# Token rows for the experts: turned a PSUM bank at a time, and the first pair's tokens by products

## The chip, the cores and the metric

One core of one Trainium2 chip runs the whole layer. The time is the device time of one execution in microseconds, as the median of several runs; 1143.99 us before the change (three runs, 1141.77 to 1146.23). Engines are named as the profile names them: PE (TensorE, products), PEld (its weight loads), DVE (VectorE), ACT (ScalarE), POOL (GpSimd), SP (SyncE, which here only issues transfers).

## What is computed

One layer of a backbone over 512 latent tokens of width 1024 (batch 1, depth 1). After the first half (retention, long convolution, merging and output projection) comes the part that matters here, the routed experts:

```
h2 = modulate(rms_norm(x, norm2_g), sh2, sc2)              # 512 x 1024
group_p = softmax(h2 @ rg_w + rg_b);  g = argmax            # 4 groups of 8 experts
in_group = the 8 logits of that group;  top 2 of softmax    # two experts for each token
y[token] = sum over its 2 experts of weight * (silu(u @ w1[e]) * (u @ w3[e])) @ w2[e]     # hidden 512
x = x + gt2 * y;  out = rms_norm(x, final_norm_g)
```

All is f32. The 32 experts' weights are 32 x 3 x 2 MB, about 201 MB, and each is read once.

## The kernel before

**Experts in pairs, pairs in groups.** The 32 experts make 16 pairs, two pairs to a group `g` (0 to 7). An expert takes up to 64 tokens in a round (`CAP`), so a pair is 128 slots: 64 of its first expert, 64 of its second. For a pair, `up_half` makes the two hidden products (`ga` with w1, `up` with w3) from the pair's tokens in columns `xg` (feature on the partition, slot along the row), `hidden` gates them, `turned` transposes the result into `hT`, `down` makes `y`, and `add` puts weighted results back to the tokens with a one-hot matrix (`co`). In the trace an f32 product or transpose of the code is two rows or one: 20 warm-up products are 40 rows, 4 transposes 4 rows, 8 products of 64x512 16 rows.

**Where the tokens come from.** `rows_of` and `chosen` build `gtm`, one-hot rows (token to slot) for the four experts of a group. `slot_sums` multiplies it with token numbers and the tokens' norm factor, `fetched` makes an index of that and fetches 128 rows of the token stream from HBM into `xr[j]` with an indirect DMA (POOL), and `scaled` multiplies each row by its token's norm factor (half on DVE, half on ACT). `token_columns` (line 1492) turns `xr` into `xg`: it transposes blocks of 128 features on PE into a PSUM bank `xg`, and after each block (one pair) or each two (two pairs) a DVE or ACT instruction, in turns, takes it out with the modulation (`am2c`, `sh2c`). So one bank is written, read, written again, and read by the other engine.

**Order of the work.** A stretch from the last output products to the first pair's tokens (`tail()` to line 1644) stands in program order on all engines (`order = tc.manual_schedule()`). From line 1667 on, PE alone keeps program order, and a scheduler orders the other engines. At the first pair the two fetches are waited for on PE with `keep_warm` products; `xr[0]` is turned, the first half of `up_half` runs, `xr[1]` is turned, the second half runs. In each group from 0 to 6 the turn for the next group's two pairs stands on PE behind the second pair's `up` and behind `turned(hh)`, ahead of the second pair's `down`.

**The weights' transfers.** `plan` lists 192 tiles of 1 MB (12 for a pair: 8 for `up`, 4 for `down`), and `ahead(n)` issues them on SP in that order as buffers come free. The buffers are 12 ring tiles (`ew`) and loans: two tiles in the former `xm`, one in two halves (`xwxe`, the second half in the pool `late`, which takes the place of the routing's scratch when that is closed), one `xwxf`; in all 16 tiles in flight or in use. A tile's buffer is free when its products are done. In group 5 a check for experts with more than 64 tokens stands in the program (`overflow`), which SP also passes.

Of the kernel before, what the change touches and what calls it, by code (L numbers as in the profile page):

```python
# [48 lines left out]
W = 4, 2, 1, 10, 2, 8  # L49
# [124 lines left out]
def body(es: ExitStack, tc: tile.TileContext, d, out, dump=None):  # L174
# [15 lines left out]
    def bank(name, tag="x"):  # L190
        return ps.tile([128, 512], F32, name=name, tag=tag, bufs=4)

    def f(t):
        return t.bitcast(F32)
# [59 lines left out]
    def run(gen):  # L254
        for _ in gen:
            pass
# [26 lines left out]
    def early_table(func, src):  # L283

        A.activation(junk1, src, func, scale=0.0)
# [953 lines left out]
    rl, sq = [], []  # L1239

    def out_tile(o, k):
        xk = xm[k // 2][:, k % 2, :]
        V.scalar_tensor_tensor(out=xk, in0=o, scalar=gt1c[:, k:k + 1], in1=xk, op0=ALU.mult, op1=ALU.add)
        s = wide("sq2")[:, 0:512]
        A.activation(s, xk, AF.Square)
        sq.append(s)
        if 0 < k < 7:
            V.tensor_tensor(out=s, in0=sq[0], in1=s, op=ALU.add)
            sq.pop(0)
# [76 lines left out]
    def tail():  # L1326
# [13 lines left out]
        early_table(AF.Sqrt, sq[-1][:, 0:1])  # L1340
        ss = bank("ss")
# [7 lines left out]
        V.tensor_tensor(out=lgt_v, in0=lgt_v, in1=rl[2][:, 0:160], op=ALU.add)  # L1349
        for j in range(2):  # L1350
            for t in range(4):
                T.matmul(ss[:, 4 * j + t:4 * j + t + 1], sq[j][:, 128 * t:128 * t + 128], ones[:, 0:1], start=True, stop=True)
        V.tensor_reduce(out=mtmp, in_=ss[:, 0:8].rearrange("p (j t) -> p t j", j=2), axis=AX.X, op=ALU.add)
# [3 lines left out]
        rsqrt_mean(mrs, mtmp, 1024, mtmp, mss)  # L1357
# [133 lines left out]

    def token_columns(xg, pairs, c0=0):

        w = 128 * len(pairs)
        for k in range(8):
            i = w * k % 512
            if i == 0:
                p = bank("xg")
            for j, pr in enumerate(pairs):
                T.transpose(p[:, i + 128 * j:i + 128 * j + 128], xr[pr][:, 128 * k:128 * k + 128], ident)  # L1500
            o = xg[k][:, c0:c0 + w]
            if k % 2:
                A.activation(o, p[:, i:i + w], AF.Identity, bias=sh2c[:, k:k + 1], scale=am2c[:, k:k + 1])  # L1503
            else:
                V.tensor_scalar(out=o, in0=p[:, i:i + w], scalar1=am2c[:, k:k + 1], scalar2=sh2c[:, k:k + 1],  # L1505
                                op0=ALU.mult, op1=ALU.add)
# [86 lines left out]
    def overflow():  # L1593
# [3 lines left out]
        with tc.If(rounds > 1, label="more"):  # L1597
            with tc.For_i(1, rounds, 1):
                V.tensor_scalar(out=later, in0=later, scalar1=float(CAP), scalar2=None, op0=ALU.add)
                with tc.For_i(0, 16, 1) as pi:  # L1600
# [9 lines left out]
                    token_columns(xg, [0])  # L1610
# [17 lines left out]
    def rows_of(g):  # L1628
        gt = wk.tile([128, 4, 4 * CAP], F32R, name="gtm", tag="gt", bufs=1)
        return gt, chosen(gt, pos[:, :, 4 * g:4 * g + 4], 4, slots, 2)  # L1630

    gt, more = rows_of(0)
    xg = column_tiles(4, "m")
    rs = []
    for j in range(2):
        next(more)
        rs.append(fetched(slot_sums(gt, 128 * j, wHL[:, :, j, 4:8]), j))
    weights_ = shares()
    next(weights_)
    keep_warm(W[5])  # L1640
    scaled(rs[0], 0)
    token_columns(xg, [0])
# [38 lines left out]
    for g in range(8):  # L1681
# [7 lines left out]
        if g == 0:  # L1689
            ab_ = [bank("ga", "acc"), bank("up", "acc")]  # L1690
            up_half(ab_, 0, xg, 0, ahead_weights)
            scaled(rs[1], 1)
            token_columns(xg, [1], 128)
            run(weights_)
# [10 lines left out]
            rs = []  # L1705
# [25 lines left out]
        if g == 0:  # L1731
            gt, more = rows_of(1)
            run(more)
            nxt = described(1, gt)
# [7 lines left out]
        if g < 7:  # L1742
            for j in range(2):
                scaled(rs[j], j)
            hT_ = turned(hh)
            xg = column_tiles(4, "m")
            token_columns(xg, [0, 1])
            parts.append((now[1][0], down(hT_, now[1][1], ahead_weights)))
# [121 lines left out]
```

## Time and profile before

| | |
|---|---|
| median of 3 runs | 1143.99 us |
| the profiled execution: its own time | 1140.63 us |
| its span, first to last instruction | 1138.9 us |
| PE, DVE, ACT busy | 95%, 51%, 30% of the span |
| moved by DMA | 289.48 MB |
| mean granted TensorE clock | 0.965 of 2.4 GHz |

The page gives busy time, slices and groups; a row of the timeline gives the start and the length of an instruction or of a run of like ones, and in brackets how long its engine was idle before it and what ended that. A matmul's end is modelled, so a PE that reads as fully busy may still be waiting a little. The span is 1.7 us shorter than the execution's own time, which is 3.4 us below the median.

### The profile page before, as it was taken

What the parts mean: (1) busy time and instruction counts of PE and PEld (TensorE: products, weight loads), DVE (VectorE), ACT (ScalarE), POOL (GpSimd) and SP (SyncE); (2) the same over time, 40 slices, a digit from 0 to 9 for tenths busy, and PEclk for the clock granted to TensorE, in tenths of its full rate; (3) what the DMA queues carried; (4) which work ended last, traced back from release to release, by engine and by line L of the source; (5) the groups of instructions that cost most, each with busy time, mean ns of one, the idle gap of its engine ahead of it and who ended that gap; (6) DMA issues with size and microseconds to landing.
All of it is one profiled execution on the core that took longest, in us unless ns stands there. A gap on an engine that the chain in (4) does not pass through costs nothing. (4 is left out here: it accounts for less than half of the span.)

```text
span 1138.9 us, 13047 instructions
## 1 busy us (share of the span) xinstructions
PE 1077.3 (95%) x4958; PEld 675.8 (59%) x4958; DVE 579.5 (51%) x1045; ACT 337.9 (30%) x588; POOL 41.1 (4%) x68
## 2 busy tenths in 40 slices
PE   6999999999999999999998798989898989898996
PEld 3667888877778777877888233534353434343343
DVE  1778995775475768865535241424243324233234
ACT  2487352445533455333332211111101010101113
POOL 0010000000000000000002000000000000000000
PEclk8999999999999999999998798989998989999899
DMA  7653343111122128883599489999999998999971
GB/s 267 197 175 110 111 142 127 62 56 60 55 91 74 38 78 298 262 274 106 199 420 397 165 314 366 418 417 415 418 416 418 417 409 351 415 417 418 418 305 74
DMA packets 64925, 289.48 MB, mean 254 GB/s; under 512 B 8086, under 2 KB 10262, under 8 KB 45274
## 3 DMA queue, kind: packets, MB, share of 16 engines
q1 hardware_dynamic: 59818, 274.51, 62.9%
q0 software_dynamic: 5040, 14.10, 3.6%
q8 instruction: 40, 0.66, 0.2%
q14 instruction: 27, 0.22, 0.1%
HBM read 288.57 MB, written 4.19 MB: 257 GB/s over the span
## 5 line engine op out<-in xcount | busy, mean ns | idle before, releaser
L198 DVE TENSOR_TENSOR wL<-raw,wH 128x512 fp32r<-128x512 f32 x142 | 97.1, 688 | 118.9 <-ACT wH L197 110.3
L197 ACT CAST wH<-raw 128x512 fp32r<-128x512 f32 x142 | 87.9, 621 | 206.6 <-PE ro L202 33.7
L1534 PE MATMUL up<-ew,xgm 128*64 128x512 f32 x496 | 111.7, 592 | 0.0
L1559 PE MATMUL y<-ew,hT 128*64 128x512 f32 x368 | 105.2, 653 | 1.0 <-DVE hT L1548 1.0
L1534 PE MATMUL ga<-ew,xgm 128*64 128x512 f32 x280 | 93.4, 619 | 0.0
L1540 DVE TENSOR_TENSOR hh<-hh,up 128x512 f32<-128x512 f32 x16 | 11.0, 688 | 135.5 <-PE up L1534 135.5
L1534 PEld LDWEIGHTS up<-ew,xgm 128*64 128x64 f32 x496 | 35.3, 137 | 71.2 <-issue 69.7
L1559 PEld LDWEIGHTS y<-ew,hT 128*64 128x64 f32 x368 | 31.5, 151 | 50.1 <-issue 48.6
L1500 PE MATMUL xg<-ident,xr 128*128 128x128 f32 x128 | 29.5, 339 | 29.5 <-DVE xgm L1505 24.6
L1490 ACT ACTIVATE xr<-xr,rs 128x512 f32<-128x512 f32 x16 | 11.5, 722 | 152.5 <-DMA xr<-rows,idx 152.5
L1565 DVE SCALAR_TENSOR_TENSOR yv<-y,wsl,gt 128x512 f32<-128x512 f32 x30 | 22.4, 747 | 64.2 <-PE y L1559 59.9
L197 ACT CAST yh<-yv 128x512 fp32r<-128x512 f32 x30 | 18.5, 618 | 104.2 <-DVE yv L1565 92.5
L1582 DVE TENSOR_TENSOR xmid<-xmid,co 128x512 f32<-128x512 f32 x58 | 39.8, 688 | 12.5 <-PE co L1574 11.9
L1574 PE MATMUL co<-yh,cmb 128*128 128x512 f32 x114 | 46.1, 405 | 0.0
L1574 PE MATMUL co<-yl,cmb 128*128 128x512 f32 x114 | 44.8, 393 | 0.0
L1534 PEld LDWEIGHTS ga<-ew,xgm 128*64 128x64 f32 x280 | 28.4, 144 | 24.0 <-issue 24.0
L1503 ACT ACTIVATE xgm<-xg,sh2c,am2c 128x256 f32<-128x256 f32 (+1 forms) x36 | 19.4, 540 | 77.7 <-PE xg L1500 77.7
L1500 PEld LDWEIGHTS xg<-ident,xr 128*128 128x128 f32 x128 | 16.3, 160 | 41.3 <-DVE xgm L1505 34.4
L342 DVE SCALAR_TENSOR_TENSOR acc<-adaw,scT,acc 128x1024 f32<-128x1024 f32 x28 | 35.6, 1282 | 8.7 <-DMA adaw<-ada 8.7
L1489 DVE TENSOR_SCALAR xr<-xr,rs 128x512 f32<-128x512 f32 x16 | 7.8, 486 | 60.9 <-DMA xr<-rows,idx 60.9
L1539 ACT ACTIVATE hh<-ga 128x512 f32<-128x512 f32 x16 | 9.6, 598 | 91.4 <-PE ga L1534 87.2
L1505 DVE TENSOR_SCALAR xgm<-xg,am2c,sh2c 128x256 f32<-128x256 f32 (+1 forms) x36 | 18.4, 512 | 32.8 <-PE xg L1500 32.8
(476 smaller groups left out, 2400.8 us busy)
## 6 DMA issues: line engine op xcount, KB each, us to landing
ew<-w SPq DMA_DIRECT2D x146, 1024.0 KB, 14.8
raw<-w_in SPq DMA_DIRECT2D x52, 512.0 KB, 3.7
xwxm<-w SPq DMA_DIRECT2D x40, 512.0 KB, 13.6
adaw<-ada SPq DMA_DIRECT2D x32, 512.0 KB, 6.0
xwxe<-w SPq DMA_DIRECT2D x22, 512.0 KB, 16.4
xwxf<-w SPq DMA_DIRECT2D x10, 1024.0 KB, 16.4
adaw<-ada SPq DMA_DIRECT2D x32, 256.0 KB, 6.0
raw<-ret_w_o SPq DMA_DIRECT2D x8, 512.0 KB, 3.7
```

What stands on the lines that cost most here:

```text
L197: A.copy(h, src)
L198: V.tensor_tensor(out=l, in0=src, in1=f(h), op=ALU.subtract)
L342: V.scalar_tensor_tensor(out=acc[i], in0=w, scalar=scT[:, k, 0:1], in1=acc[i], op0=ALU.mult, op1=ALU.add)
L1490: A.activation(xr[j][:, 512:1024], xr[j][:, 512:1024], AF.Copy, scale=rs)
L1500: T.transpose(p[:, i + 128 * j:i + 128 * j + 128], xr[pr][:, 128 * k:128 * k + 128], ident)
L1503: A.activation(o, p[:, i:i + w], AF.Identity, bias=sh2c[:, k:k + 1], scale=am2c[:, k:k + 1])
L1505: V.tensor_scalar(out=o, in0=p[:, i:i + w], scalar1=am2c[:, k:k + 1], scalar2=sh2c[:, k:k + 1], op0=ALU.mult, op1=ALU.add)
L1534: T.matmul(ab_[i][64 * e:64 * e + 64], xg[k][:, c0 + 64 * e:c0 + 64 * e + 64], w[e][q], start=(k == 0), stop=(k == 7))
L1559: T.matmul(y_[n][64 * e:64 * e + 64], hT_[:, 128 * k + 64 * e:128 * k + 64 * e + 64], w[e][2 * q + n], start=(k == 0), stop=(k == 3))
L1565: V.scalar_tensor_tensor(out=yv, in0=y_[n], scalar=wsl, in1=gt2[:, ns], op0=ALU.mult, op1=ALU.mult)
L1574: T.matmul(p, cmb[:, 128 * t:128 * t + 128], y[j][:, ns], start=(start and i + j == 0), stop=(i == len(parts) - 1 and j == 1))
L1582: V.tensor_tensor(out=xmid[:, t, ns], in0=xmid[:, t, ns], in1=p, op=ALU.add)
```

## The change

1. `token_columns` makes all transposes of one PSUM bank, and only then takes the bank out, all of it by one engine: banks 0 and 3 by DVE, 1 and 2 by ACT (one pair: bank 0 DVE, bank 1 ACT). It is now a generator that yields after each bank.
2. In groups 0 to 6, three of the four banks are turned ahead of `turned(hh)`, the fourth behind it.
3. The first pair's tokens are not fetched. DVE multiplies the pair's one-hot rows by the tokens' norm factor (`gs`, two instructions of 128x256, held in `xr[0]`), and PE multiplies the token stream `xmid` with them: 8 blocks of 4 f32 products of 128x128 into 4 banks, which DVE and ACT take out in turns. The `keep_warm` products that waited for the fetch are gone.
4. The second pair's rows are fetched as before, but their index is made between the second and the third bank of these products; they are turned only behind the first pair's `down`.
5. In `tail()` the squares' sums are added to the end on DVE, so 4 products make the sum over features and no DVE sum of two halves is left; one addition of router logits moves into the wait for the square root.

On PE at the first pair (`xr_5098` and `xr_5094` are `xr[0]`, `xr_5099` is `xr[1]`), before:

```order
L251 MATMUL warm<-ones 128x128 x4
L1475 MATMUL wsl<-wHL,gtm 128x4 x8
L251 MATMUL warm<-ones 128x128 x16
L1500 MATMUL xg<-ident,xr_5098 128x128 x8
L1534 MATMUL ga<-ew,xgm 64x512 x8
L1534 MATMUL up<-ew,xgm 64x512 x8
L1500 MATMUL xg<-ident,xr_5099 128x128 x8
L1453 LDWEIGHTS ones_b
```

and now:

```order
L251 MATMUL warm<-ones 128x128 x4
L1651 MATMUL xg<-xr_5094,xmid 128x128 x16
L1473 MATMUL wsl<-wHL,gtm 128x4 x4
L1651 MATMUL xg<-xr_5094,xmid 128x128 x16
L1451 LDWEIGHTS ones_b
...
L1538 MATMUL ga<-ew,xgm 64x512 x8
L1538 MATMUL up<-ew,xgm 64x512 x8
L1538 MATMUL ga<-ew,xgm 64x512 x8
```

The 32 products stand where the index products, 16 warm-up products and 8 transposes stood, and no transpose stands between the halves of the first pair's `up` any more.

On PE at a group's turn (here of group 1; the tiles by number, so that the four banks `xg` can be told apart; `xr0`, `xr1` hold the two pairs' rows), before:

```order
L1534 MATMUL up_5515<-ew_5281,xgm_5165 64x512
L1546 MATMUL hT_5555<-ident_61,hh_5548 128x128 x4
L1500 MATMUL xg_5564<-ident_61,xr0_5098 128x128
L1500 MATMUL xg_5564<-ident_61,xr1_5099 128x128
...
L1500 MATMUL xg_5585<-ident_61,xr0_5098 128x128
L1500 MATMUL xg_5585<-ident_61,xr1_5099 128x128
L1559 MATMUL y_5592<-ew_5283,hT_5560 64x512
```

and now:

```order
L1538 MATMUL up_5508<-ew_5294,xgm_5161 64x512
L1506 MATMUL xg_5550<-ident_61,xr0_5094 128x128
L1506 MATMUL xg_5550<-ident_61,xr1_5095 128x128
...
L1506 MATMUL xg_5564<-ident_61,xr0_5094 128x128
L1506 MATMUL xg_5564<-ident_61,xr1_5095 128x128
L1550 MATMUL hT_5571<-ident_61,hh_5541 128x128 x4
L1506 MATMUL xg_5578<-ident_61,xr0_5094 128x128
L1506 MATMUL xg_5578<-ident_61,xr1_5095 128x128
L1506 MATMUL xg_5578<-ident_61,xr0_5094 128x128
L1506 MATMUL xg_5578<-ident_61,xr1_5095 128x128
L1563 MATMUL y_5585<-ew_5296,hT_5576 64x512
```

The transposes of `hh` now have twelve of the sixteen token transposes ahead of them and four behind.

On SP behind the prefetch (`xwxe_5353` and `xwxe_5326` are the first half of the borrowed pair of half tiles, `_5354` and `_5327` the second), before:

```order
L1212 DMA xwxm<-w 128x1024 x4
L1212 DMA xwxe_5353<-w 128x1024
L1212 DMA xwxf<-w 128x2048
L1230 DMA ew<-w 128x2048 x6
L1212 DMA xwxe_5354<-w 128x1024
```

and now:

```order
L1212 DMA xwxm<-w 128x1024 x4
L1212 DMA xwxe_5326<-w 128x1024
L1212 DMA xwxe_5327<-w 128x1024
L1212 DMA xwxf<-w 128x2048
L1230 DMA ew<-w 128x2048 x12
```

The second half, which waits for the routing's scratch, now stands ahead of `xwxf` and of the ring's first reloads.

The core of the diff:

```
@@ -1244,7 +1244,7 @@
         s = wide("sq2")[:, 0:512]
         A.activation(s, xk, AF.Square)
         sq.append(s)
-        if 0 < k < 7:
+        if k:
             V.tensor_tensor(out=s, in0=sq[0], in1=s, op=ALU.add)
             sq.pop(0)
@@ -1337,8 +1337,7 @@
                 xt += [bank("xmt") for t in range(2)]
                 for t in range(2):
                     turned_tokens(t, 1, xt[t], range(2))
-        early_table(AF.Sqrt, sq[-1][:, 0:1])
-        ss = bank("ss")
+        early_table(AF.Sqrt, ident[:, 0:1])
         router_bank("rl")
         for t in range(4):
             router_part(range(4, 7), t)
@@ -1346,15 +1345,14 @@
         router_bank("rl", "acc")
         for t in range(4):
             router_part([7], t)
-        V.tensor_tensor(out=lgt_v, in0=lgt_v, in1=rl[2][:, 0:160], op=ALU.add)
-        for j in range(2):
-            for t in range(4):
-                T.matmul(ss[:, 4 * j + t:4 * j + t + 1], sq[j][:, 128 * t:128 * t + 128], ones[:, 0:1], start=True, stop=True)
-        V.tensor_reduce(out=mtmp, in_=ss[:, 0:8].rearrange("p (j t) -> p t j", j=2), axis=AX.X, op=ALU.add)
+        ss = bank("ss")
+        for t in range(4):
+            T.matmul(ss[:, t:t + 1], sq[0][:, 128 * t:128 * t + 128], ones[:, 0:1], start=True, stop=True)
         xt += [bank("xmt", "acc") for t in range(2, 4)]
         for t in range(4):
             turned_tokens(t, 1, xt[t], range(2, 4) if t < 2 else range(4))
-        rsqrt_mean(mrs, mtmp, 1024, mtmp, mss)
+        rsqrt_mean(mrs, ss[:, 0:4], 1024, mtmp, mss,
+                   lambda: V.tensor_tensor(out=lgt_v, in0=lgt_v, in1=rl[2][:, 0:160], op=ALU.add))
         for t in range(4):
             kept(t, 1, xt[t])
             dump("xm_%d" % t, xmid[:, t, :])
@@ -1489,21 +1487,27 @@
         V.tensor_scalar(out=xr[j][:, 0:512], in0=xr[j][:, 0:512], scalar1=rs, scalar2=None, op0=ALU.mult)
         A.activation(xr[j][:, 512:1024], xr[j][:, 512:1024], AF.Copy, scale=rs)
 
+    def columns_out(p, k, o, i):
+
+        if i % 2:
+            A.activation(o, p, AF.Identity, bias=sh2c[:, k:k + 1], scale=am2c[:, k:k + 1])
+        else:
+            V.tensor_scalar(out=o, in0=p, scalar1=am2c[:, k:k + 1], scalar2=sh2c[:, k:k + 1], op0=ALU.mult, op1=ALU.add)
+
     def token_columns(xg, pairs, c0=0):
 
         w = 128 * len(pairs)
-        for k in range(8):
-            i = w * k % 512
-            if i == 0:
-                p = bank("xg")
-            for j, pr in enumerate(pairs):
-                T.transpose(p[:, i + 128 * j:i + 128 * j + 128], xr[pr][:, 128 * k:128 * k + 128], ident)
-            o = xg[k][:, c0:c0 + w]
-            if k % 2:
-                A.activation(o, p[:, i:i + w], AF.Identity, bias=sh2c[:, k:k + 1], scale=am2c[:, k:k + 1])
-            else:
-                V.tensor_scalar(out=o, in0=p[:, i:i + w], scalar1=am2c[:, k:k + 1], scalar2=sh2c[:, k:k + 1],
-                                op0=ALU.mult, op1=ALU.add)
+        n = 512 // w
+        for i in range(8 // n):
+            p = bank("xg")
+            ks = range(n * i, n * i + n)
+            for k in ks:
+                for j, pr in enumerate(pairs):
+                    T.transpose(p[:, w * (k % n) + 128 * j:w * (k % n) + 128 * j + 128], xr[pr][:, 128 * k:128 * k + 128],
+                                ident)
+            for k in ks:
+                columns_out(p[:, w * (k % n):w * (k % n) + w], k, xg[k][:, c0:c0 + w], (0, 1, 1, 0)[i])
+            yield
 
     def column_tiles(n, name, tag="xg", bufs=2):
         x4 = [wk.tile([128, 4, n * CAP], F32, name="xg" + name, tag=tag, bufs=bufs) for i in range(2)]
@@ -1629,17 +1633,29 @@
         gt = wk.tile([128, 4, 4 * CAP], F32R, name="gtm", tag="gt", bufs=1)
         return gt, chosen(gt, pos[:, :, 4 * g:4 * g + 4], 4, slots, 2)
 
+
     gt, more = rows_of(0)
     xg = column_tiles(4, "m")
-    rs = []
-    for j in range(2):
-        next(more)
-        rs.append(fetched(slot_sums(gt, 128 * j, wHL[:, :, j, 4:8]), j))
+    next(more)
+    gs = xr[0][:, 0:512].rearrange("p (t s) -> p t s", t=4)
+    for t in (0, 2):
+        V.tensor_tensor(out=gs[:, t:t + 2], in0=f(gt[:, t:t + 2, 0:128]),
+                        in1=mrs[:, t:t + 2, None].to_broadcast([128, 2, 128]), op=ALU.mult)
+    next(more)
     weights_ = shares()
-    next(weights_)
-    keep_warm(W[5])
-    scaled(rs[0], 0)
-    token_columns(xg, [0])
+    rs = [None]
+    for i in range(4):
+        p = bank("xg")
+        for k in (2 * i, 2 * i + 1):
+            for t in range(4):
+                T.matmul(p[:, 128 * (k % 2):128 * (k % 2) + 128], xmid[:, t, 128 * k:128 * k + 128], gs[:, t],
+                         start=(t == 0), stop=(t == 3))
+        if i == 1:
+            rs.append(fetched(slot_sums(gt, 128, wHL[:, :, 1, 4:8]), 1))
+            next(weights_)
+        for k in (2 * i, 2 * i + 1):
+            columns_out(p[:, 128 * (k % 2):128 * (k % 2) + 128], k, xg[k][:, 0:128], i)
+    run(weights_)
     ahead(early_tiles + 2)
     order.__exit__(None, None, None)
     tc.no_sync_barrier()
@@ -1689,9 +1705,6 @@
         if g == 0:
             ab_ = [bank("ga", "acc"), bank("up", "acc")]
             up_half(ab_, 0, xg, 0, ahead_weights)
-            scaled(rs[1], 1)
-            token_columns(xg, [1], 128)
-            run(weights_)
             t1e.close()
             late = es.enter_context(tc.tile_pool(name="late", bufs=1, side="right", reuse_waits="tile"))
             ahead(early_tiles + 14)
@@ -1731,6 +1743,9 @@
         if g == 0:
             gt, more = rows_of(1)
             run(more)
+            scaled(rs[1], 1)
+            run(token_columns(xg, [1], 128))
+            rs = []
             nxt = described(1, gt)
         if g == 7:
             fn = wk.tile([128, 1024], F32, name="fn", tag="gt", bufs=1)
@@ -1742,9 +1757,11 @@
         if g < 7:
             for j in range(2):
                 scaled(rs[j], j)
+            xg = column_tiles(4, "m")
+            turn = token_columns(xg, [0, 1])
+            some(turn, 3)
             hT_ = turned(hh)
-            xg = column_tiles(4, "m")
-            token_columns(xg, [0, 1])
+            run(turn)
             parts.append((now[1][0], down(hT_, now[1][1], ahead_weights)))
     add(parts, [(2, 1), (3, 1)])
```

## Rows read from the trace of the kernel before

**Rows 1.** The page's forty slices of the span (28.5 us each): the mean busy share of the 16 DMA engines in tenths, and what they moved.

```profile
DMA  7653343111122128883599489999999998999971
GB/s 267 197 175 110 111 142 127 62 56 60 55 91 74 38 78 298 262 274 106 199 420 397 165 314 366 418 417 415 418 416 418 417 409 351 415 417 418 418 305 74
```

**Rows 2.** Busy time of the engines in stretches of the second half (us from the span's start): length, then PE, PEld, DVE, ACT and POOL busy with their instructions, then the granted TensorE clock as a share of 2.4 GHz, the DMA engines' busy share, and GB/s.

```profile
610.00:615.00 5.00, 4.28 (x39) 4.02 (x38) 3.24 (x12) 0.00 (x0) 0.81 (x1) 1.00 1.04 404
615.00:620.00 5.00, 4.43 (x21) 4.46 (x22) 3.00 (x11) 0.34 (x1) 2.15 (x2) 0.57 1.04 407
620.00:630.00 10.00, 5.16 (x23) 3.72 (x21) 1.72 (x4) 1.64 (x3) 1.48 (x2) 0.67 0.58 233
630.00:640.00 10.00, 8.95 (x31) 3.01 (x33) 2.69 (x10) 1.83 (x4) 0.00 (x0) 0.69 0.11 24
640.00:650.00 10.00, 6.88 (x28) 2.47 (x26) 2.38 (x8) 3.11 (x5) 0.00 (x0) 0.83 0.95 397
650.00:660.00 10.00, 8.96 (x52) 4.21 (x50) 4.32 (x10) 0.60 (x1) 0.00 (x0) 1.00 0.69 260
660.00:670.00 10.00, 10.00 (x56) 4.27 (x54) 4.87 (x15) 1.24 (x2) 1.57 (x2) 1.00 0.57 212
670.00:680.00 10.00, 10.00 (x50) 3.41 (x48) 2.10 (x4) 2.04 (x3) 0.67 (x1) 1.00 0.91 329
680.00:690.00 10.00, 6.18 (x31) 2.85 (x28) 3.46 (x6) 2.25 (x4) 0.00 (x0) 0.87 1.01 398
690.00:700.00 10.00, 10.00 (x40) 3.12 (x38) 2.10 (x3) 0.69 (x2) 0.00 (x0) 0.79 0.76 299
930.00:940.00 10.00, 9.36 (x33) 2.95 (x33) 1.03 (x2) 1.13 (x2) 0.00 (x0) 0.67 0.97 390
940.00:950.00 10.00, 10.00 (x48) 3.23 (x46) 3.51 (x6) 1.24 (x2) 0.00 (x0) 1.00 0.71 297
950.00:960.00 10.00, 10.00 (x49) 5.66 (x46) 3.93 (x6) 0.60 (x1) 0.00 (x0) 1.00 0.91 354
1100.00:1110.00 10.00, 10.00 (x47) 4.33 (x44) 1.95 (x4) 2.08 (x3) 1.46 (x2) 1.00 0.38 139
```

**Rows 3.** The timeline of SyncE's queue, which issues the weights' transfers: start, length of the stretch of issues, transfer and count.

```profile
616.07 0.46 SPq L1212 DMA_DIRECT2D xwxf<-w  x1
637.92 14.93 SPq L1230 DMA_DIRECT2D ew<-w  x6
652.95 0.37 SPq L1212 DMA_DIRECT2D xwxe<-w  x1
...
1071.71 5.31 SPq L1230 DMA_DIRECT2D ew<-w  x3
1079.18 15.43 SPq L1234 DMA_DIRECT2D ew<-w  x5
```

**Rows 4.** The timeline from the end of the squares' sums to the second half of the first pair: start, length, engine, line, operation, tiles, shape and count, and in brackets the engine's idle time before it with what ended it.

```profile
603.16 1.92 PE L1352 MATMUL ss<-ones,sq 128*128 128x1 f32 x16
...
612.56 1.14 PE L251 MATMUL warm<-ones 128*128 128x128 f32 x8
613.15 0.69 DVE L1466 TENSOR_TENSOR gtm<-slots,pos 128x512 fp32r<-128x512 f32 x1
...
616.32 2.05 PE L251 MATMUL warm<-ones 128*128 128x128 f32 x8
...
625.27 0.49 DVE L1489 TENSOR_SCALAR xr<-xr,rs 128x512 f32<-128x512 f32 x1 [5.62 <-DMA xr<-rows,idx]
...
632.38 5.51 PE L1534 MATMUL ga<-ew,xgm 128*64 128x512 f32 x16
...
641.25 0.33 PE L1500 MATMUL xg<-ident,xr 128*128 128x128 f32 x1
...
646.97 5.04 PE L1534 MATMUL ga<-ew,xgm 128*64 128x512 f32 x16
```

**Rows 5.** The timeline of the first turn of fetched rows, in the first group; then the turn's line over all eight groups: instructions with their least, median and longest ns, and the idle time of TensorE before them by what ended it (us, times).

```profile
678.12 3.60 PE L1534 MATMUL up<-ew,xgm 128*64 128x512 f32 x16
681.86 0.69 DVE L1540 TENSOR_TENSOR hh<-hh,up 128x512 f32<-128x512 f32 x1 [6.56 <-PE up L1534]
682.61 0.66 PE L1546 MATMUL hT<-ident,hh 128*128 128x128 f32 x4 [0.88 <-DVE hh L1540]
684.50 0.66 PE L1500 MATMUL xg<-ident,xr 128*128 128x128 f32 x4 [1.02 <-DVE xgm L1505]
688.63 0.69 PE L1500 MATMUL xg<-ident,xr 128*128 128x128 f32 x2 [0.64 <-DVE xgm L1505]
689.25 9.52 PE L1559 MATMUL y<-ew,hT 128*64 128x512 f32 x32
L1500 PEld LDWEIGHTS xg<-ident,xr x128: 138/141/231, 625.8 to 1055.0; 128*128 128x128 f32 x128
L1500 PE MATMUL xg<-ident,xr x128: 272/328/478, 625.9 to 1055.2; 128*128 128x128 f32 x128
  DVE xgm L1505: 58.9, 72
```

**Rows 6.** The timeline of the end: the last stretch of the last pair's up product, and its down products.

```profile
1103.41 3.60 PE L1534 MATMUL up<-ew,xgm 128*64 128x512 f32 x16
1116.44 7.14 PE L1777 MATMUL y<-ew,hT 128*64 128x512 f32 x32
```

More of the change, by code (lines that the diff above doesn't have):

```diff
@@ L48 @@
 FS = 4, 5, 6
-W = 4, 2, 1, 10, 2, 8
+W = 4, 2, 1, 10, 2
 def _hl(a):
@@ L1609, in overflow @@
                     xg = column_tiles(2, "x", "y", 4)
-                    token_columns(xg, [0])
+                    run(token_columns(xg, [0]))
                     def weights(stage, kc, i, e):
@@ L1633, in body @@
     xg = column_tiles(4, "m")
-    rs = []
-    for j in range(2):
-        next(more)
-        rs.append(fetched(slot_sums(gt, 128 * j, wHL[:, :, j, 4:8]), j))
-    weights_ = shares()
-    next(weights_)
-    keep_warm(W[5])
-    scaled(rs[0], 0)
-    token_columns(xg, [0])
+    next(more)
[4 more added lines that the diff above has]
+    next(more)
+    weights_ = shares()
+    rs = [None]
[11 more added lines that the diff above has]
+    run(weights_)
     ahead(early_tiles + 2)
@@ L1704, in body @@
             hT_ = turned(hh)
-            rs = []
         else:
```

## Prediction

> **What bounds the kernel now.** I read the slices first, then the stretches of the second half, then SP's queue, and only then the instructions of the two places that the change touches. The slices say that from about 700 us to the end the transfers run at one speed, 415 to 418 GB/s, with two dips [rows 1]; the stretches say that this is full: a share of 1.01 at 398 and 407 to 404 GB/s at 1.04 [rows 2]. The weights are 201 MB, so 418 GB/s needs 482 us for them, whatever the engines do. Yet PE is not seen to wait for a transfer: it idles at the turn, where each transpose after the first of a bank waits until the last one has been taken out. Over all eight groups that is 58.9 us in 72 waits [rows 5]. So two limits lie close together: a PE chain that is a little late, and transfers that are full most of the time. What the change is worth is decided by how far PE may move before it meets the transfers.
>
> **How far the transfers let PE move.** The last stretch of `up` uses the 187th and 188th tile and starts at 1103.41 [rows 6]. Behind these two, SP issues four more MB in five pieces [rows 3], and the transfers end at 1103.8 (a share of 0.38 of ten us from 1100 on [rows 2]). Four tiles of 1.049 MB at 418 GB/s take 10.0 us, so tile 188 lands near 1093.8: it lies ready for 9.6 us. Every us of PE beyond these 9.6 counts only if the transfers too end earlier. They can, by what they idle in the second half [rows 2]: 4.2 + 8.9 = 13.1 us from 620 to 640, where all 16 buffers are full and SP waits until 637.92 for the first `ga` to free one [rows 3]; 0.5 + 3.1 + 4.3 + 0.9 + 0 + 2.4 = 11.2 from 640 to 700, where buffers come free late; 0.3 + 2.9 + 0.9 = 4.1 from 930 to 960, around the check for overfull experts. In all 28.4 us.
>
> **The change, part by part.** *Squares' sums:* 16 rows in 1.92 us become 8, one short DVE sum goes, and a DVE addition lies beside the router's products [rows 4]: about 1 us earlier on the path to the routing. *First pair:* the one-hot rows are ready at 613.15 + 0.69 - 1.0 = 612.8. Two DVE instructions over half as many columns as the one-hot row's 0.69 take 0.7 together: 613.5. Then 32 products, two rows each. A row of the same shape is 1.14 / 8 = 0.143 us beside a granted clock of 1.00 (2.4 GHz), and 2.05 / 8 = 0.256 in the stretch granted 0.57, mostly 1.2 GHz [rows 2, 4]. That makes 9.1 or 16.4 us. I take 9.1: PE now works without a gap from 613.5 on, where it used to wait for the index twice before the clock fell. With 1.2 us for the index products and the counts, `ga` starts at 624 (631 at the low clock) instead of 632.38. Taking out is in banks of its own and hides beside the products; the fetch and its scaling at 625.27 leave the path. The first two `ga` stretches took 5.51 and 5.04 us against 3.60 for a like one at 2.4 GHz [rows 4, 6]: 1.9 + 1.4 gained. *Second pair's turn:* the 5.7 us between 641.25 and 646.97 leave [rows 4], and come back behind the first `down` as something between 1.0 (eight transposes at 0.13) and 5.7 (all as now); I take 2.7, since half of the taking out is on ACT and the turn's waits are gone, but DVE has this pair's `yv` ahead of it, and the index of the next fetches stands behind it on DVE and so comes later too; those rows have a whole `up`, 14 us, to land. The second pair's own rows are fetched about 2 us later than now and have 30 us. By then PE is 8.4 + 3.3 + 3.0 = 14.7 us early.
>
> *The seven turns:* now from the end of `up` at 681.72 to `y` at 689.25, 7.5 us [rows 5]. Afterwards 12 transposes run while `hh` is made (four take 0.66 with the last one's drain of 0.27, so 0.13 each: 1.6 us), the four of `hh` and their copy of 0.7 follow, and the fourth bank fits beside that copy: `y` starts about 3.1 us after `up`, 4.4 us are saved, 31 in seven. The two `y` stretches behind a turn take 9.52 us, not 7.2, since the clock is granted at 0.79 there [rows 2, 5]; whether these 2.3 come back I leave open (0 to 16 us in all).
>
> PE alone could so end 46 to 62 us earlier. It won't: it meets the weights.
>
> *SP's queue:* the second half tile `xwxe` waits for the routing's scratch, near 624, and `xwxf`, issued at 616.07 before, is now behind it. The prefetch therefore runs dry about 2.5 us sooner, near 623.3, and starts again near 627.5: 4 us idle instead of 13.1, for by then the first `ga` has freed its tiles (624 + 3.6). From 640 to 700 the buffers come free 10 to 16 us earlier, and I leave 2 of the 11.2. At the check I leave 2 of 4.1, since SP's own stop there stays while the queue ahead of it is fuller. That is 8 idle instead of 28.4.
>
> **Sum.** The transfers end 20.4 us earlier, the slack of 9.6 is used up, and what follows tile 188 (1138.9 - 1103.4 = 35.5 us) stays as it is: 1138.9 - 30.0 = 1108.9 us of span, 1110.6 in that execution's own time of 1140.63. The median shown is 3.4 above that execution, so on the median 1114.0. The bounds: 3 to 14 us idle at the restart (14 if the products run at the low clock throughout) and 0 to 4 at the check give 1109 to 1126.
>
> One rule bears on the full share. Rows 1 and 2 show 415 to 418 GB/s wherever the share is 1.01. The Trainium skill (DMA: Bandwidth & Descriptors, "Where 436 GB/s comes from") puts the ceiling of a core's sixteen ports at 435 GB/s; by that figure, as an estimate, the last 450 us of transfers would take 18 us less and the sum would be 1096. No slice of rows 1 goes above 420, so I keep 418.
>
> **Rivals.** *The clock falls once PE waits for weights* (chance 0.14). A stretch of two tiles takes PE 3.6 us and the transfers 5.0, so near the end PE idles a third of the time, and the stretches at and behind a turn, where it idled over a third, are the ones granted 0.67 to 0.87 [rows 2]. Against it: at the low clock a stretch takes 5 to 6 us, PE falls behind, stops idling, and the clock returns. Price: the last `up`, the closing sums and the last `down` (1103.4 to 1123.6, 20 us) at up to half speed, of which I count 10: 1124. The Trainium skill (TensorE: Matmul & The Clock Gate, "Loop structure matters more than you think") warns of just this loop, which waits for a transfer between products and runs cold; the trace agrees as far as the turns' 9.52 for 7.2 go, though those waits are for DVE and ACT.
>
> *The bank's wait stays* (0.08). If a transpose must still wait for the bank before it, or the fourth bank for the first, the turns save nothing: 1138.9 - 14.7, the transfers not binding, 1124.2, on the median 1129. Against it: every wait in the trace is within one bank [rows 5].
>
> *Transfers do not bind* (0.05): they speed up or PE's buffers last. Then PE's own 46 to 62 us count: about 1090. Eight slices in a row at 415 to 418 GB/s, 228 us, speak against it [rows 1].
>
> *Slower: products whose loads are not hidden* (0.07). The place is the first pair. The longest single transpose took 0.478 and its load 0.231 [rows 5]; if each of the 64 rows costs both, 0.709, the products last 45.4 us, `ga` starts at 660, 27.7 later than now, and SP's queue with it. Of the 30 us, 20.8 remain (9.6, 9.2 from 640 to 700, 2 at the check), while the first stretches stay slow: 1138.9 + 27.7 - 20.8 + 3.3 = 1149, on the median 1154. It decides from 0.6 us a row on. Against it: 0.256 is the dearest row of this shape in a run.
>
> **How the numbers follow.** The forecast has 0.66, the rivals 0.34. A difference under 0.5% (5.7 us) is about what a measurement of this kernel can't tell from no change. Faster: 0.66 + 0.14 + 0.08 + 0.05, less 0.02 for their upper ends, 0.91; slower 0.05, the rest of the last rival and those ends, 0.04, no change. The range 1103 to 1132 takes in the forecast's bounds, and below it a little for a fuller restart, and the clock and bank rivals above; it leaves out the free transfers, the slow products and some of the tails.
>
> **What would show it.** Right: `ga` near 624 with a granted clock of 1.00; idle of the transfers under 5 us between 620 and 640 and a full share from 660 on; 3 to 3.5 us from `up` to `y` at each turn, with no TensorE wait on `xgm`; PE waiting for `ew` in the last groups; transfers ending near 1083. Wrong: a product row above 0.2 us, a share under 0.95 after 700, waits on `xgm` that stay, or a tail of more than 36 us behind the last `up`.

## The result, and the profile after

The changed kernel takes 1110.71 us (median of four runs, 1109.82 to 1112.55) beside 1143.1 before: a ratio of 0.9715, interval 0.969 to 0.9739. Forecast were 1114.0 and a range of 1103 to 1132. The profiled execution has a span of 1110.8 us; forecast were 1108.9. The tables and sums below are in spans.

**The transfers** first. The page's slices, which answer to [rows 1]:

```profile
DMA  7652343121122116876299899999999998999992
GB/s 274 199 181 96 114 152 131 57 76 58 58 76 76 38 55 234 278 241 217 76 376 414 324 357 412 417 419 416 418 417 417 417 419 333 421 419 415 418 405 96
```

Stretches of ten us, which answer to [rows 2] (the last three columns are the granted clock, the DMA share and GB/s):

```profile
620.00:630.00 10.00, 10.00 (x65) 5.47 (x65) 5.68 (x22) 4.04 (x8) 2.61 (x3) 1.00 0.50 161
650.00:660.00 10.00, 9.26 (x47) 3.67 (x49) 4.98 (x16) 2.13 (x4) 2.47 (x2) 1.00 0.76 256
900.00:910.00 10.00, 7.22 (x33) 2.34 (x31) 3.37 (x6) 1.24 (x2) 0.00 (x0) 1.00 1.01 420
920.00:930.00 10.00, 9.69 (x42) 6.59 (x38) 6.38 (x10) 0.00 (x0) 0.00 (x0) 1.00 0.73 302
930.00:940.00 10.00, 8.98 (x50) 4.24 (x52) 3.95 (x14) 0.00 (x0) 1.99 (x2) 1.00 0.82 310
1080.00:1090.00 10.00, 10.00 (x37) 5.27 (x37) 1.62 (x3) 0.00 (x0) 1.46 (x2) 1.00 0.47 176
```

The reader sees the transfers idle 5.0 us at the restart, where the prefetch has run dry and the ring's reloads begin (620 to 640; 13.1 before), 2.4 from 650 to 660 (11.2 from 640 to 700 before) and 2.7 + 1.8 = 4.5 at the check (4.1 before); they end near 1085 instead of 1103.8. From 660 on nothing else is below a full share. At 900 it is PE that idles, 2.8 of 10 us, at a granted clock of 1.00.

**The first pair** on PE (timeline, columns as in [rows 4]):

```profile
603.25 1.87 PE L1350 MATMUL ss<-ones,sq 128*128 128x1 f32 x8
607.57 5.80 PE L251 MATMUL warm<-ones 128*128 128x128 f32 x40
613.21 0.22 PE L1414 MATMUL cum<-asg,tri 128*128 128x128 bf16 x1
615.32 3.81 PE L1651 MATMUL xg<-xr,xmid 128*128 128x128 f32 x32 [0.81 <-DVE xr L1642]
619.33 3.82 PE L1651 MATMUL xg<-xr,xmid 128*128 128x128 f32 x32
623.16 3.65 PE L1538 MATMUL ga<-ew,xgm 128*64 128x512 f32 x16
```

A row of a product costs 3.81 / 32 = 0.119 us, and `ga` starts at 623.16 instead of 632.38.

**The first turn** (timeline), beside [rows 5]:

```profile
665.67 1.53 PE L1506 MATMUL xg<-ident,xr 128*128 128x128 f32 x12
667.04 0.60 PE L1550 MATMUL hT<-ident,hh 128*128 128x128 f32 x4
667.63 0.63 PE L1506 MATMUL xg<-ident,xr 128*128 128x128 f32 x4
668.42 7.09 PE L1563 MATMUL y<-ew,hT 128*64 128x512 f32 x32 [0.17 <-DVE hT L1552]
```

and, from the view of the transposes' line over all groups, how long they waited for a bank to be taken out (us, times):

```profile
  DVE xgm L1495: 0.3, 1
```

From the end of `up` (665.74) to `y` are 2.68 us, at every turn 2.68 to 2.76, where it was 7.04 to 8.19 before (the means of the seven are 2.69 and 7.65). The 58.9 us in 72 waits are 0.3 in one.

**The end**: the last `up` and `y` (timeline), beside [rows 6]:

```profile
1075.29 3.65 PE L1538 MATMUL up<-ew,xgm 128*64 128x512 f32 x14 [0.40 <-DMA ew<-w]
1088.37 7.14 PE L1794 MATMUL y<-ew,hT 128*64 128x512 f32 x32
```

and the waits of the products from 640 us on (us in total, times, longest):

```profile
PE up L1538 <- DMA ew<-w: 12.7, 10, 2.3
PE ga L1538 <- DMA ew<-w: 7.7, 7, 1.4
```

PE now waits 20.4 us for weights, before 0; the last `up` itself waits for `ew`, so the slack of 9.6 us is gone. From the start of its last 14 rows to the end are 1110.8 - 1075.29 = 35.5 us, as before.

### The profile page after: what moved, and what is told of

Read it like the earlier page. It is cut to its first block, busy times and chain, and to the rows that moved or that the text cites. A ratio compares the mean times of both kernels' runs of the same rounds, so it can differ in the third digit from the quotient of the medians.

```text
span 1110.8 us, 13072 instructions
## 1 busy us (share of the span) xinstructions
PE 1062.9 (96%) x4970; PEld 675.2 (61%) x4970; DVE 577.4 (52%) x1044; ACT 334.5 (30%) x587; POOL 40.4 (4%) x67
## 2 busy tenths in 40 slices
DMA packets 64781, 289.22 MB, mean 260 GB/s; under 512 B 8006, under 2 KB 10182, under 8 KB 45130
## 5 line engine op out<-in xcount | busy, mean ns | idle before, releaser
L1538 PE MATMUL up<-ew,xgm 128*64 128x512 f32 x496 | 127.2, 602 | 12.8 <-DMA ew<-w 12.7
L1563 PE MATMUL y<-ew,hT 128*64 128x512 f32 x368 | 93.6, 595 | 1.8 <-DVE hT L1552 1.8
L1538 PEld LDWEIGHTS up<-ew,xgm 128*64 128x64 f32 x496 | 38.7, 138 | 92.1 <-issue 65.8
L342 DVE SCALAR_TENSOR_TENSOR acc<-adaw,scT,acc 128x1024 f32<-128x1024 f32 x28 | 35.7, 1282 | 11.4 <-DMA adaw<-ada 11.3
L198 DVE TENSOR_TENSOR yl<-yv,yh 128x512 fp32r<-128x512 f32 x30 | 20.8, 692 | 19.9 <-ACT yh L197 19.9
L1538 PE MATMUL ga<-xwxe,xgm 128*64 128x512 f32 x64 | 29.4, 594 | 0.0
L1481 POOL DMA_INDIRECT xr<-rows,idx x15 | 15.5, 1033 | 364.4 <-DVE wsl L1528 352.8
L1578 PEld LDWEIGHTS co<-yh,cmb 128*128 128x128 f32 x114 | 21.4, 188 | 10.6 <-PE up L1538 4.1
```

Source lines behind the costliest of these rows:

```text
L198: V.tensor_tensor(out=l, in0=src, in1=f(h), op=ALU.subtract)
L342: V.scalar_tensor_tensor(out=acc[i], in0=w, scalar=scT[:, k, 0:1], in1=acc[i], op0=ALU.mult, op1=ALU.add)
L1481: G.indirect_dma_start(out=xr[j], out_offset=None, in_=rows, in_offset=bass.IndirectOffsetOnAxis(ap=idx, axis=0), bounds_check=511, oob_is ...
L1538: T.matmul(ab_[i][64 * e:64 * e + 64], xg[k][:, c0 + 64 * e:c0 + 64 * e + 64], w[e][q], start=(k == 0), stop=(k == 7))
L1563: T.matmul(y_[n][64 * e:64 * e + 64], hT_[:, 128 * k + 64 * e:128 * k + 64 * e + 64], w[e][2 * q + n], start=(k == 0), stop=(k == 3))
L1578: T.matmul(p, cmb[:, 128 * t:128 * t + 128], y[j][:, ns], start=(start and i + j == 0), stop=(i == len(parts) - 1 and j == 1))
```

## The experiments

The theory: the weights' transfers bind now, and the time is their idle plus a constant. The main rival: the chain on PE sets the time, and waits for weights are only slack. Ratios are to the kernel before, measured beside it; executions of one kernel differ by 1 to 6 us (the change: 1109.82 to 1112.55), so a difference of 2 us between two of these kernels is not one that their times show. The edits are cut to the lines that matter, and some statements are put on one line.

**One part alone: the turns.** The kernel before with the new `token_columns` and three banks ahead of `hh`.

```
-            token_columns(xg, [0, 1])
+            turn = token_columns(xg, [0, 1]); some(turn, 3); hT_ = turned(hh); run(turn)
```

> Only the turns change (a bank at a time, one engine for each bank, three banks ahead of hh); the first pair is fetched and the squares are summed as before. Theory (the weights' transfers bind once PE is early): up to the first turn nothing is earlier, so the transfers keep their 21.9 us of idle between 620 and 680; only the 2.4 us from 690 to 700 and the 9.6 us of slack can be gained: 1138.9 - 12 = 1127 of span, about 1131 on the median, ratio near 0.989. Rival (the PE chain sets the time, seven turns of 4.4 us each count in full): 1138.9 - 31 = 1108, about 1112, ratio 0.973. The turns themselves take about 3 us from up to y by both.

Measured: 1117.82 us, ratio 0.978 (0.973 to 0.983), between the two. The expectation had overlooked that the first pair's turns use the same function; on PE:

```profile
626.25 1.94 PE L1508 MATMUL xg<-ident,xr 128*128 128x128 f32 x8 [4.58 <-DVE xr L1489]
628.11 4.35 PE L1540 MATMUL ga<-ew,xgm 128*64 128x512 f32 x16
```

The eight transposes take 1.9 us to `ga` where they took 6.5, the second half's turn goes the same way, and the transfers idle 7.5 us at the restart instead of 13.1. Of the 9 us by which `ga` starts earlier after the whole change, this gives 4; the rest of the change, above all products in place of the fetch, gives the other 5. The run does not separate the theories, so the seven group turns were changed alone:

```
+            xg = column_tiles(4, "m"); turn = bank_columns(xg, [0, 1])   # the groups' turns only
+            some(turn, 3); hT_ = turned(hh); run(turn)
```

> The kernel before with the seven turns of the groups changed alone; the first pair's two turns stay as before (a bank emptied by both engines in turns), which the kernel with the turns only had changed too. Theory (the weights' transfers bind): nothing is earlier up to the first group's turn, so the 21.9 us of idle from 620 to 680 stay, and only 2.4 us (690 to 700) and the 9.6 us of slack can be gained: about 1127 of span, 1131 on the median, ratio 0.989. Rival (the PE chain sets the time): 1138.9 - 31 = 1108, about 1112, ratio 0.973.

Measured: 1130.94 us, ratio 0.9899 (0.9873 to 0.9924). The theory's number, 19 us from the rival's. Its transfers stand still at the restart as before:

```profile
620.00:630.00 10.00, 2.21 (x9) 1.06 (x7) 1.31 (x3) 1.18 (x2) 1.93 (x3) 0.62 0.62 249
630.00:640.00 10.00, 8.44 (x31) 2.82 (x31) 3.10 (x11) 2.29 (x5) 0.01 (x1) 0.70 0.07 14
650.00:660.00 10.00, 9.62 (x48) 4.20 (x44) 2.51 (x8) 0.60 (x1) 0.00 (x0) 0.84 0.52 190
```

Its turns are 2.68 us as well, and yet only 11.5 us come of the 31: PE waits 17.1 us for weights in it.

**The other part alone: first pair and squares**, with the groups' turns as before.

```
-            turn = token_columns(xg, [0, 1]); some(turn, 3); hT_ = turned(hh); run(turn)
+            hT_ = turned(hh); xg = column_tiles(4, "m"); old_columns(xg, [0, 1])
```

> The first pair by products and the squares' sums as in the change; the turns of the groups as before (engines in turns, behind hh). Theory: PE is 16 us early from the first turn on (its up ended at 681.7 before and at 665.7 after the change), the turns cost 7.5 us again, the transfers' idle of the start is gone, so PE and not the weights bind: 1138.9 - 16 = 1123, about 1127 on the median, ratio 0.986; PE waits for ew under 5 us in all, for xgm about 50. Rival (the weights bind from the restart on, the turns are worth nothing): as the change, about 1111, ratio 0.9715.

Measured: 1126.64 us, ratio 0.9855 (0.9808 to 0.9903), as the theory has it. The old turn's line shows the bank's wait back, and PE waits 0.0 us for weights:

```profile
  DVE xgm L1525: 48.7, 56
```

So neither part gives the whole: the groups' turns give 11.5 us alone, first pair and squares 16.5, and the change 32.4. The groups' turns are worth 11.5 us with a late restart and 15.9 with an early one.

**All four banks behind `hh`.**

```
-            some(turn, 3)
             hT_ = turned(hh)
             run(turn)
```

> As the change, but all four banks are turned behind the transposes of hh instead of three ahead. Each of the seven turns should take about 2 us longer on PE (1.6 us of transposes and part of a bank's taking out no longer lie beside the making of hh), 14 us in all. Theory (transfers bind): hidden, since PE waits for ew and so on some 30 us in the last groups: 1110 to 1114, ratio to before 0.971 to 0.975, with PE's waits for weights shorter by about 14 us. Rival (the PE chain sets the time): about 1125, ratio 0.984.

Measured: 1111.52 us, ratio 0.9734 (0.9682 to 0.9786). The turns are 3.2 us, not the 4.7 that the expectation comes to: `hT` waits 0.9 for `hh`, and 16 transposes in one piece take 1.91.

```profile
665.80 0.66 PE L1550 MATMUL hT<-ident,hh 128*128 128x128 f32 x4 [0.89 <-DVE hh L1544]
666.29 1.91 PE L1506 MATMUL xg<-ident,xr 128*128 128x128 f32 x16
668.13 4.08 PE L1563 MATMUL y<-ew,hT 128*64 128x512 f32 x18
```

Of the 4.9 us by which a turn became shorter (mean of the seven), turning and taking out a bank at a time gives 4.4 and the three banks ahead about 0.5. How much of the 4.4 comes of writing a whole bank first, and how much of one engine for each bank, no run separates. The 3.9 us in seven turns are too little to tell theory from rival by time.

**More tiles ahead of the check for overfull experts.**

```
-OA = 4
+OA = 12
```

> As the change, but SP may issue 12 tiles of weights instead of 4 ahead of the check for overfull experts (the pair of borrowed tiles is kept out of that stretch). PE's own instructions stay. Theory (transfers bind): the 4.5 us that the transfers idle between 920 and 940 go, and the time with them: about 1106, ratio 0.968. Rival (the PE chain sets the time, waits for weights are only slack): 1111, ratio 0.9715, no change against the change.

Measured: 1111.89 us, ratio 0.9723 (0.9676 to 0.977): the rival's number. But the idle had not gone, which the theory's number rests on; it had moved:

```profile
930.00:940.00 10.00, 9.96 (x54) 4.53 (x56) 3.73 (x13) 0.30 (x1) 1.98 (x2) 1.00 1.01 408
940.00:950.00 10.00, 10.00 (x48) 3.30 (x46) 3.38 (x6) 2.91 (x5) 0.00 (x0) 1.00 0.83 342
950.00:960.00 10.00, 9.79 (x52) 4.66 (x48) 3.21 (x6) 2.00 (x5) 0.00 (x0) 1.00 0.78 301
```

and from 880 to 960 SP itself waited (us in total, times, longest):

```profile
SPq L1601 <- SPq L1601: 18.4, 5, 8.4
```

SP stands 18.4 us in the branch (19.4 in the change, 7.7 before). The trace has eight semaphore events of SP there, at 923.0 to 930.8 in the change and 940.9 to 951.0 here. The transfers run out beside them, in the change and here:

```profile
930.00:931.00 1.00, 0.00 (x0) 0.00 (x0) 0.52 (x2) 0.00 (x0) 0.00 (x0) 1.00 0.07 16
951.00:952.00 1.00, 1.00 (x8) 0.32 (x6) 0.00 (x0) 0.00 (x0) 0.00 (x0) 1.00 0.00 0
```

and SP's next issues stand at 930.90 and 951.15: it lets what is in flight land, and only then issues again. Before, SP had been waiting for PE to free buffers and stood for less long; eight more tiles ahead of the check made it stand no longer than in the change.

**The check in the last group**, where only three tiles are issued behind it, and **no check at all**. (The stretch that leaves the two borrowed `xm` tiles out moves with the check.)

```
-OV = 10
-OA = 4
+OV = 14
+OA = 13
```

> As the change, but the check for overfull experts stands in the last group (14 pairs done) instead of pair 10, with 13 more tiles issued ahead of it, so that only the last three tiles are issued behind it. The kernel with 12 tiles ahead of the check moved the idle from 920-940 to 940-960 without gaining: on SP the branch past the check waits for all eight of SP's transfer queues, that is until what is in flight has landed, so it empties the pipe wherever it stands. Theory: at the end nothing that the last up needs is behind it, so the 4.5 us of idle go and the time with them: 1106, ratio 0.9675. Rival (PE sets the time, or the last three tiles now come late for the last down): 1111 or more.

Measured: 1107.67 us, ratio 0.9696 (0.9666 to 0.9725), an interval that takes in the change's 0.9715; the time alone doesn't decide. The idle is gone:

```profile
920.00:930.00 10.00, 10.00 (x55) 8.27 (x56) 7.80 (x16) 0.00 (x0) 0.23 (x1) 1.00 1.01 419
930.00:940.00 10.00, 10.00 (x48) 3.38 (x50) 2.84 (x9) 0.72 (x1) 1.74 (x2) 1.00 1.02 410
```

```
-GENERAL = True
+GENERAL = False
```

> As the change, without the check for overfull experts and the rounds behind it (left out: experts with more than 64 tokens). Theory (what the check costs is the emptying of the transfers, 4.5 us): as with the check in the last group, 1106 to 1108. Rival (the branch costs PE, DVE and ACT too, in the last group as in the sixth): 1 to 3 us faster than that, 1104 to 1105.

Measured: 1108.24 us, ratio 0.9708 (0.9688 to 0.9728): as the late check, and not the rival's 1104 to 1105. So what the check costs fits the emptying of the transfers, and at the end, where SP still stands 15.8 us, it costs nothing that shows. By the ratios it is worth 0.8 to 2.2 us, by the medians 2.5 to 3, at the edge of what these runs can tell.

**Less to fetch.** Every fourth tile from the 65th on is fetched half.

```
-                S.dma_start(w, src)
+                n_ = 1024 if i >= 64 and i % 4 == 0 else 2048
+                S.dma_start(w[:, 0:n_], src[:, 0:n_])
```

> As the change, but from the 65th tile on every fourth tile is fetched only half (32 times 0.5 MB left out, the products use the fetched half twice, so PE's work is the same and the output is not the reference's). 16.8 MB at 418 GB/s are 40 us of transfers. Theory (transfers bind in the last groups): the waits of PE for ew go, some 23 us from 840 on, and PE sets the time: 1088 to 1094. Rival (the PE chain sets the time already): 1111.

Measured: 1101.72 us, ratio 0.9641 (0.9609 to 0.9673). The page counts 284.50 MB instead of 289.22, so 4.72 MB or 11.3 us were left out, not 40: the tiles with `i % 4 == 0` are mostly borrowed ones, which the edit passes by. The span fell by 11.2 us for 11.3 us of transfers. With `i % 4 == 3` instead:

> The kernel with less to fetch hit only nine ring tiles (4.7 MB, 11.3 us of transfers), since most of its numbers fell on borrowed tiles, and PE still waited for ew. Here the tiles are those with number 3 of 4, all in the ring: 31 halves from the 65th tile on, 16.3 MB or 39 us at 418 GB/s (the products use the fetched half twice, the output is not the reference's). Theory (the weights' transfers bind, PE alone could end some 22 us earlier, its idle from 820 to 1080): waits for ew near 0 and 1086 to 1093. Rival (PE binds as well, the tail and the buffers leave no more): 1100 or more.

Measured: 1079.19 us, ratio 0.9468 (0.9448 to 0.9488), faster than either expected. Its `up` products, by the groups by shape:

```profile
L1539 PE MATMUL up<-ew,xgm 128*64 128x512 f32 x496 | 112.1, 592 | 0.0
```

With no wait for weights left, PE alone ends at 1075.2: 63.7 us before the old span, where the prediction had put 46 to 62. Of these the changed kernel has 28.1; the other 35.6 go to waiting for transfers. The two runs with less to fetch and the group turns alone lie far from the rival's numbers, and they decide between it and the theory.

**An earlier restart.** `xwxf` is issued ahead of `xwxe`, and the experts' shares (the DVE chain that frees the routing's scratch) run ahead of and in the first pair's products.

```
     rs = [None]
+    next(weights_)
...
     ahead(early_tiles + 2)
+    ready[early_tiles + XF] = borrowed(...)   # in the ordered stretch, behind xwxm
```

> As the change, but the borrowed 1 MB tile xwxf is issued ahead of the halves xwxe, and the shares of the experts (the DVE chain that ends in nrounds and frees the routing's scratch) run ahead of and in the first pair's products instead of behind them. The transfers now idle 5.0 us between 620 and 630 because SP waits for nrounds until 626.3; xwxf issued near 616 gives them 2.5 us more, nrounds near 622.6 another 1. Theory (every us of idle of the transfers counts): 2 to 4 us faster than the change, 1107 to 1109. Rival (PE sets the time): ga starts no earlier, 1111.

Measured: 1111.24 us, ratio 0.9724 (0.9698 to 0.9749): no gain that shows.

```profile
620.00:630.00 10.00, 10.00 (x57) 4.79 (x58) 2.38 (x10) 3.82 (x7) 1.97 (x3) 1.00 0.95 369
640.00:650.00 10.00, 8.74 (x50) 3.88 (x46) 4.92 (x13) 2.64 (x6) 0.00 (x0) 1.00 0.89 347
650.00:660.00 10.00, 10.00 (x52) 3.84 (x54) 4.08 (x12) 1.45 (x2) 2.46 (x2) 1.00 0.64 208
```

4.5 us of idle go from 620 to 630, and 2.3 come back from 640 to 660, where SP waits for products to free a buffer (10.4 us for one `ga`, 9.6 for one `y`). There PE still binds, and the transfers can't run further ahead of it.

**Fewer warm-up products**, and **all three together** (late check, early restart, fewer warm-up products).

```
-W = 4, 2, 1, 10, 2
+W = 4, 2, 1, 7, 2
```

> As the change, but 14 instead of 20 warm-up products stand behind the router's last ones, ahead of the running sums cum. In the change the one-hot of the experts (asg) is done at 611.65 and cum at 613.21, because the warm-up products last until 613.37; that is where the squares' 1 us went. Theory: cum starts when asg is there, the products and ga start 1.0 to 1.5 us earlier, and SP and the buffers with them: 1109.3, ratio 0.9705. Rival: the clock falls without these products (granted 0.5 near 615), the 64 rows of products cost up to 0.24 instead of 0.12 us each: 1111 to 1118.

Measured: 1111.03 us, ratio 0.9735 (0.9722 to 0.9748), no gain; the timeline shows the rival:

```profile
606.38 3.29 PE L251 MATMUL warm<-ones 128*128 128x128 f32 x28
611.78 0.23 PE L1414 MATMUL cum<-asg,tri 128*128 128x128 bf16 x1 [2.11 <-DVE asg L1409]
613.90 6.62 PE L1651 MATMUL xg<-xr,xmid 128*128 128x128 f32 x32 [0.81 <-DVE xr L1642]
620.72 3.82 PE L1651 MATMUL xg<-xr,xmid 128*128 128x128 f32 x32
624.56 3.65 PE L1538 MATMUL ga<-ew,xgm 128*64 128x512 f32 x16
```

The products start 1.4 us earlier, but behind 2.11 us of idle; from 610 to 620 the granted clock is 0.66 of 2.4 GHz, the first 32 rows take 6.62 us instead of 3.81, and `ga` starts 1.4 us later than in the change.

> Together: the check in the last group, xwxf ahead of xwxe with the shares early, and 14 warm-up products. Issuing earlier at the restart alone moved the idle of the transfers from 620-630 to 640-660, where the buffers are full and wait for PE; with PE 1.2 us earlier some of it should come off. Theory: 1107.7 of the late check less 1 to 3: 1105 to 1107, ratio 0.967. Rival (each gain is eaten at the end by PE's own tail): 1107 to 1109.

Measured: 1107.24 us, ratio 0.9705 (0.9689 to 0.9721), with the same 6.6 us products. It and the late check alone are the fastest kernels that fetch all the weights, by their medians some 3 us below the change, by their ratios 1 to 2; their intervals and that of the change overlap.

The idle of the transfers (for each ten us from 620 to 700 and from 880 to 980, ten times what the share lacks of 1.01) beside the span:

| kernel | idle | span | against the change: idle, span |
|---|---|---|---|
| the change | 12.4 | 1110.8 | |
| group turns alone | 28.8 | 1128.5 | +16.4, +17.7 |
| all turns alone | 16.7 | 1116.1 | +4.3, +5.3 |
| all four banks behind | 10.5 | 1109.4 | -1.9, -1.4 |
| 12 tiles ahead of the check | 10.7 | 1109.9 | -1.7, -0.9 |
| early restart | 10.0 | 1109.5 | -2.4, -1.3 |
| fewer warm-up products | 12.9 | 1112.3 | +0.5, +1.5 |
| no check | 6.9 | 1107.4 | -5.5, -3.4 |
| all three together | 7.5 | 1107.9 | -4.9, -2.9 |
| late check | 6.6 | 1105.3 | -5.8, -5.5 |

Idle and span are of the same, profiled execution, which lies up to 3 us from its kernel's median; the rows within 2 us of the change tell little by themselves, and the two with the turns alone and the three without idle at the check carry the reading. Within 2.1 us the span follows the idle, wherever the idle lies. The exceptions among the kernels with all the weights are those in which PE doesn't wait for weights: the kernel before (29.4, 1138.9) and first pair alone (14.8, 1121.9).

## Why the prediction was right

The mechanism held: PE meets the weights, the slack of 9.6 is used up, the tail of 35.5 stays, and what is left is how much less the transfers idle. Its sum missed the span by 1.9 us, and that is closer than its terms were: 3.9 us more of idle than forecast were partly made up by 2.6 us that no run assigns. By its steps:

- **Products at the first pair.** Taken at 9.1 us, measured 7.6 (0.119 us a row, not 0.143); `ga` at 623.16, not 624. The other bound was real: with 14 warm-up products instead of 20 the low clock came, and half of the rows took 0.207 us each.
- **Squares' sums.** About 1 us earlier was forecast. From the sums' start [rows 4] to `cum` (612.40 in the trace before) it was 9.24 us. After, the profiled execution has 9.96; the granted clock was 0.50 there from 604 to 610, and the 8 rows took 1.87 us. The eight other kernels with the same sums and 20 warm-up products have 1.05 to 1.32 for these rows and 7.6 to 8.4 us to `cum`. The gain is there, 0.9 to 1.6 us; in the profiled execution it doesn't show. The expectation of the run with fewer warm-up products read that one execution as a rule, and was wrong.
- **Second pair's turn.** 2.7 taken. Its eight transposes take 1.1; from the first `y`'s end to the next `ga` are about 2.3 us more than before, 1.26 of them a wait of PE for ACT to take a bank out.
- **The seven turns.** 3.1 us from `up` to `y` taken, 2.68 measured, and the 2.3 us of clock at `y` came back as well (7.09 us for its 32 rows, not 9.52), so PE alone gained 63.7 us, more than the 46 to 62 that it was given. That this moved the time so little is because the transfers bind.
- **Transfers' idle**, the term that decides. 8 us were left, 11.9 measured: 5.0 for 4 at the restart, 2.4 for 2 behind it, 4.5 for 2 at the check. The last is the mis-sized one. The prediction took SP's stop as a time in which a fuller queue goes on feeding the transfers; the runs show a drain, which waits for just that queue. The low bound of 1109 also takes the 2 us behind the restart away, which its sentence doesn't say; with the terms that it names the bounds are 1111 to 1126. That the end still came only 1.3 us later than forecast (1085 for 1083.4) leaves those 2.6 us.
- **The clock rival.** It did not set the time, but it came once. PE waits for weights for over a quarter of the time in some stretches (7.22 busy of 10), and the granted clock is 1.00 there, as in every ten us from 610 to 1100 but one (0.83 from 950 to 960). That one holds the longest wait, and the 14 rows of `up` behind it take 5.34 us instead of 3.65:

```profile
953.95 5.34 PE L1538 MATMUL up<-ew,xgm 128*64 128x512 f32 x14 [2.31 <-DMA ew<-w]
955.00:957.00 2.00, 2.00 (x8) 0.68 (x6) 0.00 (x0) 0.00 (x0) 0.00 (x0) 0.50 0.99 414
```

From 959 on the clock is back at 1.00, and the next wait for weights is 0.50 us where 1.3 to 1.4 are usual: PE was late, waited less, and the loss doesn't show at the end. So the prediction's argument against this rival held. Behind the usual waits of 1.3 to 1.4 us the clock stayed, and in the kernel with the early restart it stayed behind one of 2.17. The Trainium skill (TensorE: Matmul & The Clock Gate, "Loop structure matters more than you think") warns of a loop with long waits for transfers between products; this trace agrees behind the one wait of 2.31 us, and not behind the others.

- **Bank's wait, free transfers, slow products.** None came: one wait of 0.3 us; 20.4 us of waits for weights; 0.119 us a row. (Against free transfers the prediction counts eight slices in a row at 415 to 418 GB/s; [rows 1] has seven, 199 us, which argue the same.) The Trainium skill (Perfetto Trace Analysis, "Matmuls") has products rotate through banks so that taking out overlaps the next ones; the trace agrees, with 58.9 us of waits gone.

The median came 3.3 us below the forecast although the span came 1.9 above, and that is luck of the execution: the prediction had carried over the 3.4 us by which the profiled execution of before lay under its median, and that of after (1112.55) lies 1.8 above its own.

## What to carry to other kernels

Before pricing a saving on the engine that reads as busy, price how far it may move until it meets the transfers, and then count only what the transfers idle less. Two savings that meet the same limit don't add: 11.5 and 16.5 us alone gave 32.4 here, as one opened the room for the other (the group turns alone leave the transfers 13.1 us idle at the restart, the change 5.0). Look whether a control-flow check on the queue that issues transfers drains them, as it did here, and put it where nothing urgent is queued behind it; here that gave 1 to 3 us, not clear of the spread of the runs.

## What was not expected of the hardware

- A branch on SP past an unused block left the transfers idle for 4 to 5 us at both places of the full stream where it stood (near 930 and near 950) in the kernels whose PE waits for weights, and held SP for 18 to 20 us with all the weights to fetch; before, where SP had been waiting for PE's products, it held SP for 7.7 and the idle was 4.1.
- In both kernels that left 12 warm-up rows out, PE idled 2.1 us ahead of the first pair's products, and half of these then took 0.207 us a row instead of 0.119: the rows that fill the gap cost nothing that shows. Two profiles don't make a rule of it: 32 warm-up rows behind the same two gaps (0.29 and 1.01 us) took 6.76 us before, 5.15 with all turns alone and 3.82 with the group turns alone.
- At each turn 20 transposes in a row stand between the products, and the granted clock stays 1.00. The Trainium skill (TensorE: Matmul & The Clock Gate, "Part 4: PE-mode transpose") says that transposes don't engage the full clock; here they didn't cost it.
